# Gated MLP of an encoder layer: the down projection by Strassen's scheme, seven products for eight, with block sums on GpSimd

## The chip, the cores and the metric

The kernel runs on one core of a Trainium2 chip. The metric is the device time of one execution in microseconds (us). The core has a matrix engine (TensorE; PE in the profile, and PEld for its weight loads), VectorE (DVE), ScalarE (ACT), GpSimd (POOL), SyncE (SP), which issues the loads, and sixteen DMA engines. Every engine takes its own instructions in their order and waits for the others by semaphores.

## The reference

Two layers (`DEPTH = 2`) over 512 positions of width 1024; each has attention beside a gated convolution, a gated MLP, and an embedding gate. The change touches the last line of the MLP:

```python
h = rmsnorm(x, g_ffn[i])
u = dwconv(h @ w_up[i], w_ffn_conv[i])        # width 2 * D_FF, D_FF = 2816
a, val = u[..., :D_FF], u[..., D_FF:]
x = x + (jax.nn.silu(a) * val) @ w_down[i]    # (512, 2816) @ (2816, 1024)

h = rmsnorm(x, g_ple[i])
pg = jax.nn.sigmoid((h @ w_ple_gate[i]).astype(jnp.float32)).astype(x.dtype)
x = x + pg * (p[i] @ w_ple[i])
```

All is float32. The kernel gets near that precision by splitting each operand into a rounded high part and the rest (`split`, `weight`) and taking three products for one (`mm3`: high by high, high by low, low by high).

## The kernel before

**Tiles.** The residual stream `xs` stays in SBUF as 4 tiles of 128 tokens. The normed stream is transposed into `hh` and `hl` (high and low), hidden rows on the partitions. Every weight is loaded as 128x1024 numbers (512 KB) into `raw` (3 buffers); ScalarE casts it to `wh` and VectorE writes the rest into `wl` (5 buffers each, used in turn). So a weight's split has to wait until the tile that used the buffer five weights earlier is multiplied.

**Up projection.** The 22 blocks of 128 hidden columns are taken in order `j`. Each needs two weight tiles (`i = 2j` for the gate, `2j + 1` for the value) and for each 8 x 3 matmuls of 128x512 into a PSUM tile, `ps_mm` and `ps_sc` in turn (two buffers each): I call these 24 matmuls an up tile. `taps` makes the width 3 convolution of it (one ScalarE and two VectorE instructions, into `fa`), ScalarE applies Silu to the gate, VectorE multiplies both and the result is split into `gth` and `gtl`.

**Down projection.** `CHUNKS` cuts the 22 blocks into 8, 8 and 6. After the up tiles of a chunk `proj` runs over the two halves of 512 output columns and the four token tiles; for each it adds up `len(ks)` x 3 matmuls in one PSUM tile (`ps_tp`, three buffers, in the last chunk `ps_mm` and `ps_sc`), and `residual` adds the tile to `xs` on VectorE. In the last chunk `norm` follows for each token tile, whose square root is the only GpSimd work of this part.

**Order.** The program is written as loops, and a scheduler with a model of the engines' times then sets each engine's order. TensorE therefore runs parts of a later up tile or token tile ahead of a wait where the scheduler saw one. PSUM tiles and SBUF buffers of one tag are used in turn.

Of the kernel before, what the change touches and what calls it, by code (L numbers as in the profile page):

```python
# [11 lines left out]
F32 = mybir.dt.float32  # L12
F32R = mybir.dt.float32r
BF16 = mybir.dt.bfloat16
I32 = mybir.dt.int32
AF = mybir.ActivationFunctionType
ALU = mybir.AluOpType
AX = mybir.AxisListType

P = 128  # L20
L = 2
S = 512
NT = S // P
D = 1024
KD = D // P
# [10 lines left out]
FF = 2816  # L36
NJ = FF // P
EPS = 1e-6
CHUNKS = ((0, 8), (8, 16), (16, 22))
MAGIC = 12582912.0  # L40
LAG1 = 2
LAG2 = 3
# [16 lines left out]
def encoder_kernel(ctx, tc, x_in, pT, pos, inv, w_a1, w_z, w_g, w_uq, w_ukv, w_au, w_cu, w_o,  # L59
# [15 lines left out]
    def psum(tag="mm"):  # L75
        return ps.tile([P, S], F32, tag=tag, name="ps_" + tag, bufs={"mm": 2, "av": 1, "sc": 2, "tp": 3}[tag])

    def weight(src, n=1024):
        raw = wp.tile([P, n], F32, tag="raw", name="raw", bufs=3)
        nc.sync.dma_start(raw, src)  # L80
        h = wp.tile([P, n], F32R, tag="wh", name="wh")
        lo = wp.tile([P, n], F32R, tag="wl", name="wl")
        nc.scalar.copy(h, raw)  # L83
        nc.vector.tensor_sub(lo, raw, h.bitcast(F32))  # L84
        return h, lo

    def mm3(o, st, mv, start, stop):
        nc.tensor.matmul(o, st[0], mv[0], start=start, stop=False)  # L88
        nc.tensor.matmul(o, st[0], mv[1], start=False, stop=False)  # L89
        nc.tensor.matmul(o, st[1], mv[0], start=False, stop=stop)  # L90

    def split(hi, lo, src):
        nc.scalar.copy(hi, src)  # L93
        nc.vector.tensor_sub(lo, src, hi.bitcast(F32))  # L94
# [19 lines left out]
    def norm(t, g, pool):  # L114
        junk = pool.tile([P, D], BF16, tag="junk", name="junk", bufs=1)
        ms = sm.tile([P, 1], F32, tag="ms", name="ms")
        nc.scalar.activation(junk, xs[:, t, :], AF.Square, scale=1.0 / 32.0, accum_out=ms)  # L117
        r = rsqrt_eps(ms, 1)
        for half in range(2):
            c = slice(half * 512, half * 512 + 512)  # L120
            ht = pool.tile([P, 512], F32, tag="ht", name="ht", bufs=3)
            nc.vector.scalar_tensor_tensor(ht, xs[:, t, c], r, g[:, c], ALU.mult, ALU.mult)
            tp = psum("tp")
            for j in range(4):
                nc.tensor.transpose(tp[:, j * P:(j + 1) * P], ht[:, j * P:(j + 1) * P], ident)  # L125
            dst = (slice(None), t, slice(half * 4, half * 4 + 4), slice(None))
            split(hh[dst], hl[dst], tp.rearrange("p (j q) -> p j q", j=4))
# [60 lines left out]
    def layer(l, first):  # L188
# [69 lines left out]
        def ws(o, w, rhs, nk, width, off, cols=slice(0, S), ks=None):  # L258
            for k in range(nk) if ks is None else ks:
                c = slice(k * width + off, k * width + off + P)  # L260
                mm3(o, (w[0][:, c], w[1][:, c]), (rhs[0](k, cols), rhs[1](k, cols)), k == 0, k == nk - 1)
# [249 lines left out]
        def proj(lhs, ks, ws_, after, tags):  # L511
            for n in range(2):
                wt = [weight(ws_[n * (KTOT // 2) + k // 2]) for k in ks if k % 2 == 0]
                for t in range(NT):
# [5 lines left out]
                        mm3(o, (lhs[0](k, tk), lhs[1](k, tk)), (wh[:, c], wl[:, c]), i == 0, i == len(ks) - 1)  # L520
                    after(t, n, o)

        def residual(t, n, o):
            c = slice(n * 512, n * 512 + 512)
            nc.vector.tensor_tensor(xs[:, t, c], xs[:, t, c], o, ALU.add)  # L525
# [17 lines left out]
        def taps(i, o):  # L543
            a = t2("fa")
            nc.scalar.activation(a, o, AF.Copy, scale=wfc[:, i, 1:2])
            nc.vector.scalar_tensor_tensor(a[:, 1:], o[:, :-1], wfc[:, i, 0:1], a[:, 1:], ALU.mult, ALU.add)
            nc.vector.scalar_tensor_tensor(a[:, :-1], o[:, 1:], wfc[:, i, 2:3], a[:, :-1], ALU.mult, ALU.add)  # L547
            return a

        KTOT = NJ  # L550
        NE = 3
        ew = [weight(w_up[l, i]) for i in range(NE)]
        eo = [psum("sc" if i % 2 else "mm") for i in range(NE)]
# [2 lines left out]
            for i in range(NE):  # L556
                ws(eo[i][:, c], ew[i], hT, KD, P, 0, c)
        g3 = load_gain(l, 2, ff)
        for j0, j1 in CHUNKS:
            gt = {}  # L560
            for j in range(j0, j1):
                av = []
                for i in (2 * j, 2 * j + 1):
                    if i < NE:
                        o = eo[i]
                    else:
                        w = weight(w_up[l, i])
                        o = psum("sc" if i % 2 else "mm")
                        ws(o, w, hT, KD, P, 0)
                    a = taps(i, o)  # L570
                    if i % 2 == 0:
                        nc.scalar.activation(a, a, AF.Silu)  # L572
                    av.append(a)
                nc.vector.tensor_tensor(av[1], av[0], av[1], ALU.mult)  # L574
                if j % 2 == 0:
                    gt[j // 2] = (ff.tile([P, 2, S], F32R, tag="gt", name="gth", bufs=16),
                                  ff.tile([P, 2, S], F32R, tag="gt", name="gtl", bufs=16))
                split(gt[j // 2][0][:, j % 2, :], gt[j // 2][1][:, j % 2, :], av[1])

            def after_d(t, n, o, last=(j1 == NJ)):  # L580
                residual(t, n, o)
                if last and n == 1:
                    norm(t, g3, ff)

            proj((lambda k, c: gt[k // 2][0][:, k % 2, c], lambda k, c: gt[k // 2][1][:, k % 2, c]),
                 range(j0, j1), w_down[l], after_d, ("mm", "sc") if j1 == NJ else ("tp",))

        ph = ff.tile([P, 2, S], F32R, tag="gt", name="ph", bufs=16)
        pl = ff.tile([P, 2, S], F32R, tag="gt", name="pl", bufs=16)
        raw = wp.tile([P, 1024], F32, tag="raw", name="raw", bufs=3)  # L590
        nc.sync.dma_start(raw, pT[l])
        split(ph, pl, raw.rearrange("p (k s) -> p k s", k=2))
        pw = [ff.tile([P, D], F32, tag="gt", name="pw", bufs=16) for t in range(NT)]

        KTOT = 2

# [32 lines left out]
def _layout(i):  # L629
    f = {n: np.asarray(a) for n, a in i.items()}  # L630
    w_in = f["w_in"]
    o_cb, o_cc, o_cx, o_g = A1, A1 + CW, A1 + 2 * CW, A1 + 3 * CW

    def mtiles(w):
        l, k, n = w.shape
        return w.reshape(l, k // P, P, n // P, P).transpose(0, 3, 2, 1, 4)

    def interleave(*ws):
        return np.stack([mtiles(w) for w in ws], 2)

    def halves(w):
        l, k, n = w.shape
        return w.reshape(l, k // 256, 2, P, 2, 512).transpose(0, 4, 1, 3, 2, 5).reshape(l, k // 128, P, 1024)

    z = interleave(w_in[:, :, o_cc:o_cx], w_in[:, :, o_cx:o_g], w_in[:, :, o_cb:o_cc])
    g = interleave(w_in[:, :, o_g:o_g + D], w_in[:, :, o_g + D:])
    uq = f["w_uq"].reshape(L, QL, H, DQK)
    uq = np.concatenate([uq[..., :DN].reshape(L, QL, H * DN), uq[..., DN:].reshape(L, QL, H * DR)], -1)
    ukv = f["w_ukv"].reshape(L, KVL, H, 2, 64).transpose(0, 1, 3, 2, 4).reshape(L, KVL, 1024)

    def up2(w):
        l, k, n = w.shape
        return w.reshape(l, k // P, P, n // 256, 256).transpose(0, 3, 2, 1, 4).reshape(l, n // 256, P, 1024)

    up = interleave(f["w_up"][:, :, :FF], f["w_up"][:, :, FF:])
    fc = f["w_ffn_conv"].reshape(L, 3, 2, NJ, P).transpose(0, 4, 3, 2, 1).reshape(L, P, 2 * NJ, 3)
    res = {
        "x": f["x"][0],
        "pT": f["p"][:, 0].transpose(0, 2, 1).reshape(L, 2, P, S).transpose(0, 2, 1, 3).reshape(L, P, 1024),
        "pos": f["positions"].reshape(NT, P).T.astype(np.int32),  # L660
        "inv": (np.float32(10000.0) ** (-np.arange(0, DR, 2, dtype=np.float32) / np.float32(DR)))[None],
        "w_a1": _ktile(w_in[:, :, :A1], 2).reshape(L, 4, P, 2 * A1),
        "w_z": z.reshape(L, 12, P, 1024),
        "w_g": g.reshape(L, 16, P, 1024),
        "w_uq": uq.reshape(L, 2, P, H * DQK),
        "w_ukv": ukv,
        "w_au": up2(f["w_attn_up"]),
        "w_cu": up2(f["w_conv_up"]),
        "w_o": halves(f["w_o"]),
        "w_up": up.reshape(L, 2 * NJ, P, 1024),  # L670
        "w_down": halves(f["w_down"]),
        "w_pg": halves(f["w_ple_gate"]),
        "w_ple": halves(f["w_ple"]),
        "b_gate": f["b_gate"].reshape(L, 16, P).transpose(0, 2, 1),
        "g_norm": np.stack([f["g_mix"], f["g_ffn"], f["g_ple"]], 1),
        "g_lat": np.concatenate([f["g_q_lat"], f["g_kv_lat"]], 1),
        "g_nope": np.stack([f["g_q_head"][:, :DN], f["g_k_head"][:, :DN]], 2),
        "g_rope": np.stack([f["g_q_head"][:, DN:], f["g_k_head"][:, DN:]], 1),
        "w_conv": f["w_conv"].reshape(L, 3, NC, P).transpose(0, 3, 2, 1),
        "w_fconv": fc,  # L680
    }
    return {n: np.ascontiguousarray(a) for n, a in res.items()}
# [18 lines left out]
```

## Time and profile before

| | us |
|---|---|
| median of 3 timed runs | 1575.96 (1575.94 to 1576.26) |
| span of the profiled execution, first to last instruction | 1574.1 |
| PE busy / PEld busy | 1557.1 / 1280.1 |
| DVE busy / ACT busy / POOL busy | 870.4 / 684.4 / 103.0 |
| share of PE in the chain that ended last | 94% |
| MLP of the first layer in the span | about 375 to 740 |

The page gives the profiled execution's span and not the little that lies around it; I take the 1.9 us between the span and the median for that. A busy time counts a stretch in which an engine had any instruction running; matmuls follow each other before the one ahead has ended. In rows in order of time, the first number is the start in us from the span's start, the second the duration; brackets hold the idle time of that engine ahead and what ended it. In rows of one line's instructions, the three numbers after the count are shortest, median and longest duration in ns.

### The profile page before, as it was taken

How to read it: one execution, taken by the hardware profiler on the slowest of the kernel's cores; microseconds unless marked ns; L12 is line 12 of the kernel's file. 1: busy time of each engine (PE TensorE's matmuls, PEld its weight loads, DVE VectorE, ACT ScalarE, POOL GpSimd, SP SyncE). 2: the span in 40 equal slices, each digit the busy share in tenths (PEclk: the TensorE clock that was granted, in tenths of full speed). 3: DMA queues.
4: the chain of work that ended last, by engine and by line, in shares of the span. 5: the costliest groups of instructions: out<-in, count | busy, mean ns of one | idle time of the engine just before them, and what ended most of it. 6: DMA issues, size and time to landing. Idle time of an engine off the chain costs nothing.

```text
span 1574.1 us, 18521 instructions
## 1 busy us (share of the span) xinstructions
PE 1557.1 (99%) x7288; PEld 1280.1 (81%) x7288; DVE 870.4 (55%) x1228; ACT 684.4 (43%) x1088; POOL 103.0 (7%) x153
## 2 busy tenths in 40 slices
PE   7999999999999999999999999999999999999998
PEld 6888888888888888888888888888888888888886
DVE  7787553436544553555477775443565446535543
ACT  5678732325322431334464886222344234324342
POOL 2800000000000000001055000000000000000010
PEclk9999999999999999999999999999999999999999
DMA  6211122323213221323242102232232222232222
GB/s 205 93 55 41 54 94 94 106 69 129 95 61 130 93 95 58 132 96 94 71 133 81 41 28 92 81 107 81 85 118 94 94 94 94 80 107 94 94 68 79
DMA packets 41430, 142.06 MB, mean 90 GB/s; under 512 B 5761, under 2 KB 6273, under 8 KB 41345
## 3 DMA queue, kind: packets, MB, share of 16 engines
q1 hardware_dynamic: 41344, 140.90, 27.2%
q8 instruction: 57, 0.93, 0.2%
q14 instruction: 29, 0.23, 0.0%
HBM read 138.78 MB, written 2.10 MB: 90 GB/s over the span
## 4 chain that ended last, share of the span: by engine, by line
PE 94%; POOL 2%; DVE 2%; ACT 1%; DMA 1%; issue 1%; SPq 0%; DVEq 0%; POOLq 0%; ACTq 0%
PE ps_mm L89 14%; PE ps_mm L88 14%; PE ps_mm L90 14%; PE ps_sc L89 11%; PE ps_sc L88 11%; PE ps_sc L90 11%; PE ps_tp L89 4%; PE ps_tp L88 4%; PE ps_tp L90 4%; PE ps_tp L428 2%; PE ps_tp L125 1%; POOL rs L99 1%; PE ps_av L440 1%; PE ps_av L439 1%; PE ps_tp L394 1%; PE ps_av L88 1%
## 5 line engine op out<-in xcount | busy, mean ns | idle before, releaser
L84 DVE TENSOR_TENSOR wl<-raw,wh 128x1024 fp32r<-128x1024 f32 (+1 forms) x250 | 304.0, 1217 | 325.1 <-ACT wh L83 322.7
L83 ACT CAST wh<-raw 128x1024 fp32r<-128x1024 f32 (+1 forms) x250 | 260.8, 1046 | 425.6 <-PE ps_tp L90 120.3
L88 PE MATMUL ps_mm<-hh,wh 128*128 128x512 f32 (+1 forms) x832 | 326.4, 392 | 0.5 <-DVE ycv L355 0.5
L89 PE MATMUL ps_mm<-hl,wh 128*128 128x512 f32 (+1 forms) x832 | 322.9, 388 | 0.0
L90 PE MATMUL ps_mm<-hh,wl 128*128 128x512 f32 (+1 forms) x832 | 322.5, 388 | 0.0
L90 PEld LDWEIGHTS ps_mm<-hh,wl 128*128 128x128 f32 x832 | 156.6, 188 | 34.7
L88 PEld LDWEIGHTS ps_mm<-hh,wh 128*128 128x128 f32 x832 | 156.7, 188 | 33.2 <-DVE ycv L355 1.0
L89 PEld LDWEIGHTS ps_mm<-hl,wh 128*128 128x128 f32 x832 | 156.9, 189 | 32.5 <-DVE hl L94 0.4
L89 PE MATMUL ps_sc<-hl,wh 128*128 128x512 f32 (+1 forms) x368 | 142.2, 386 | 0.0
L90 PE MATMUL ps_sc<-hh,wl 128*128 128x512 f32 (+1 forms) x368 | 142.2, 386 | 0.0
L88 PE MATMUL ps_sc<-hh,wh 128*128 128x512 f32 (+1 forms) x368 | 142.1, 386 | 0.0
L98 POOL TENSOR_SCALAR ms<-ms 128x1 f32<-128x1 f32 (+2 forms) x40 | 15.8, 394 | 1389.0 <-ACT junk L117 1360.0
L89 PE MATMUL ps_tp<-wl,gth 128*128 128x512 f32 x256 | 100.6, 396 | 0.0
L90 PE MATMUL ps_tp<-wh,gtl 128*128 128x512 f32 x256 | 100.6, 395 | 0.0
L88 PE MATMUL ps_tp<-wh,gth 128*128 128x512 f32 x256 | 99.9, 395 | 0.0
L88 PEld LDWEIGHTS ps_sc<-hh,wh 128*128 128x128 f32 x368 | 69.3, 188 | 15.3
L90 PEld LDWEIGHTS ps_sc<-hh,wl 128*128 128x128 f32 x368 | 69.3, 188 | 15.3
L89 PEld LDWEIGHTS ps_sc<-hl,wh 128*128 128x128 f32 x368 | 69.3, 188 | 15.3
L93 ACT CAST gth<-fa 128x512 fp32r<-128x512 f32 x44 | 27.3, 620 | 120.1 <-DVE fa L574 120.1
L525 DVE TENSOR_TENSOR xs<-xs,ps_tp 128x512 f32<-128x512 f32 x32 | 21.6, 685 | 85.0 <-PE ps_tp L90 85.0
L572 ACT ACTIVATE fa<-fa 128x512 f32<-128x512 f32 x44 | 27.8, 632 | 88.5 <-DVE fa L547 88.5
L88 PEld LDWEIGHTS ps_tp<-wh,gth 128*128 128x128 f32 x256 | 48.1, 188 | 11.6
(242 smaller groups left out, 2671.2 us busy)
## 6 DMA issues: line engine op xcount, KB each, us to landing
raw<-in_w_up_dram SPq DMA_DIRECT2D x88, 512.0 KB, 3.5
raw<-in_w_down_dram SPq DMA_DIRECT2D x44, 512.0 KB, 3.4
raw<-in_w_g_dram SPq DMA_DIRECT2D x32, 512.0 KB, 3.5
raw<-in_w_z_dram SPq DMA_DIRECT2D x24, 512.0 KB, 3.5
raw<-in_w_o_dram SPq DMA_DIRECT2D x16, 512.0 KB, 3.5
raw<-in_w_pg_dram SPq DMA_DIRECT2D x16, 512.0 KB, 4.2
raw<-in_w_au_dram SPq DMA_DIRECT2D x8, 512.0 KB, 3.5
raw<-in_w_cu_dram SPq DMA_DIRECT2D x8, 512.0 KB, 3.5
```

What stands on the lines that cost most here:

```text
L83: nc.scalar.copy(h, raw)
L84: nc.vector.tensor_sub(lo, raw, h.bitcast(F32))
L88: nc.tensor.matmul(o, st[0], mv[0], start=start, stop=False)
L89: nc.tensor.matmul(o, st[0], mv[1], start=False, stop=False)
L90: nc.tensor.matmul(o, st[1], mv[0], start=False, stop=stop)
L93: nc.scalar.copy(hi, src)
L98: nc.gpsimd.tensor_scalar_add(ms, ms, EPS)
L99: nc.gpsimd.tensor_tensor(r, ms, negh[:, :n], ALU.pow)
L125: nc.tensor.transpose(tp[:, j * P:(j + 1) * P], ht[:, j * P:(j + 1) * P], ident)
L428: nc.tensor.transpose(tp[:, k * P:(k + 1) * P], pe[:, k * P:(k + 1) * P], ident)
L525: nc.vector.tensor_tensor(xs[:, t, c], xs[:, t, c], o, ALU.add)
L572: nc.scalar.activation(a, a, AF.Silu)
```

## The change

The first two blocks of a layer are projected as before. The other 20 form five chunks of four. In a chunk the left matrix is cut into token halves (256 tokens) and row halves (blocks 0 and 2, blocks 1 and 3: `v[:, 0]`, `v[:, 1]` of each pair), the weights into row and column halves (`b11` to `b22`). Seven products of 256 tokens, two row blocks and 512 columns replace eight. Their operands are:

- `combos`: per pair of blocks four sums of 128x256 on GpSimd (`ss`), two of which need the one before them, and the splits of three plain and four summed operands into `ah` and `al`;
- `seven`: four sums of 128x1024 on GpSimd over the weight tiles (`t3` and in place in `b12`, `b11`, `b21`), seven weight splits, then the products in the order `r2`, `r1`, `r3`, and accumulated further `r1`, `r3`, `r1`, `r1`. The state after a product is added to `xs` each time it is an output's share, so `residual` runs 14 times a chunk.

`r2` and `r3` lie in one `ps_tp` and the one `ps_av` tile, `r1` in two `ps_tp` tiles (in the last chunk `ps_sc` and `ps_mm`). The host stores `w_down` in the blocks that `seven` loads; the bytes loaded are the same.

```diff
-CHUNKS = ((0, 8), (8, 16), (16, 22))
+CHUNKS = ((0, 2), (2, 6), (6, 10), (10, 14), (14, 18), (18, 22))
+HS = S // 2
...
+        def combos(pool, v):
+            a11, a12, a21, a22 = v[:, 0, :HS], v[:, 1, :HS], v[:, 0, HS:], v[:, 1, HS:]
+            s = pool.tile([P, 4, HS], F32, tag="ss", name="ss", bufs=2)
+            g = nc.gpsimd
+            g.tensor_tensor(s[:, 0], a21, a22, ALU.add)
+            g.tensor_tensor(s[:, 2], a11, a21, ALU.subtract)
+            g.tensor_tensor(s[:, 1], s[:, 0], a11, ALU.subtract)
+            g.tensor_tensor(s[:, 3], a12, s[:, 1], ALU.subtract)
+            h, lo = (pool.tile([P, 7, HS], F32R, tag="gt", name=n, bufs=8) for n in ("ah", "al"))
+            split(h[:, 0:2], lo[:, 0:2], v[:, :, :HS])
+            split(h[:, 2], lo[:, 2], a22)
+            split(h[:, 3:], lo[:, 3:], s)
+            return h, lo
...
+        def seven(pool, ops, blocks, add, done, tags):
+            b11, b12, b21, b22 = (pool.tile([P, 1024], F32, tag="rawd", name=n, bufs=5)
+                                  for n in ("b11", "b12", "b21", "b22"))
+            for i, b in ((2, b21), (0, b11), (1, b12), (3, b22)):
+                nc.sync.dma_start(b, blocks[i])
+            t3 = pool.tile([P, 1024], F32, tag="rawd", name="t3", bufs=5)
+            g = nc.gpsimd
+            w21 = wsplit(b21)
+            w11 = wsplit(b11)
+            g.tensor_tensor(t3, b22, b12, ALU.subtract)
+            g.tensor_tensor(b12, b12, b11, ALU.subtract)
+            wt1 = wsplit(b12)
+            g.tensor_tensor(b11, b11, t3, ALU.add)
+            wt2 = wsplit(b11)
+            g.tensor_tensor(b21, b21, b11, ALU.subtract)
+
+            def product(o, a, w, first):
+                for tt in range(2):
+                    tk = slice(tt * P, (tt + 1) * P)
+                    for i, (h, lo) in enumerate(ops):
+                        c = slice(i * 512, i * 512 + 512)
+                        mm3(o[tt], (h[:, a, tk], lo[:, a, tk]), (w[0][:, c], w[1][:, c]),
+                            first and i == 0, i == len(ops) - 1, not first)
...
+            r2 = [psum(tags[2]), psum(tags[3])]
+            product(r2, 1, w21, True)
+            out(r2, 0, 0)
+            r1 = [psum(tags[0]), psum(tags[1])]
+            product(r1, 0, w11, True)
+            out(r1, 0, 0)
+            r3 = [psum(tags[2]), psum(tags[3])]
+            product(r3, 3, wt1, True)
+            out(r3, 1, 1)
+            product(r1, 4, wt2, False)
+            out(r1, 0, 1)
+            w22 = wsplit(b22)
+            product(r3, 6, w22, False)
...
+            if c:
+                seven(ff, ops, w_down[l, 4 * c - 2:4 * c + 2], residual,
+                      (lambda t: norm(t, g3, ff)) if last else (lambda t: None),
+                      ("mm", "mm", "sc", "sc") if last else ("tp", "tp", "tp", "av"))
```

What this makes of the engines' orders is shown for the end of a chunk's up tiles, the place on which the prediction rests. First TensorE before, in the down projection of the first chunk: `gth_3894` and `gtl_3895` are the last pair of blocks. The rows are numbers 42 to 49 of its matmuls.

```order
L90 MATMUL ps_tp_4022<-wh_3992,gtl_3895 128x512
L88 MATMUL ps_tp_4048<-wh_3974,gth_3475 128x512
L88 MATMUL ps_tp_3996<-wh_3992,gth_3894 128x512 [waits Activation_49]
L89 MATMUL ps_tp_3996<-wl_3993,gth_3894 128x512
L88 MATMUL ps_tp_4022<-wh_3992,gth_3894 128x512
L90 MATMUL ps_tp_3996<-wh_3992,gtl_3895 128x512 [waits DVE_49]
L89 MATMUL ps_tp_4022<-wl_3993,gth_3894 128x512
L90 MATMUL ps_tp_4022<-wh_3992,gtl_3895 128x512
```

TensorE now, in the second chunk of four (the others of a layer but the last have the same order): `ps_tp_4403` and `ps_av_4404` are `r2`, `ps_tp_4419` and `ps_tp_4420` are `r1`, `ps_tp_4435` is the first tile of `r3`; `ah_4366` and `al_4367` belong to the last pair of blocks, `ah_4208` to the pair before it. The first two rows are matmuls 11 and 12 of the products.

```order
L90 MATMUL ps_tp_4420<-wl_4388,ah_4208 128x512
L91 MATMUL ps_tp_4420<-wh_4387,al_4209 128x512
L89 MATMUL ps_tp_4403<-wh_4383,ah_4366 128x512 [waits Activation_49]
L90 MATMUL ps_tp_4403<-wl_4384,ah_4366 128x512
L89 MATMUL ps_av_4404<-wh_4383,ah_4366 128x512
L90 MATMUL ps_av_4404<-wl_4384,ah_4366 128x512
L89 MATMUL ps_tp_4419<-wh_4387,ah_4366 128x512
```

Eight rows on, the low part of the pair is read, and then the third product begins:

```order
L91 MATMUL ps_tp_4403<-wh_4383,al_4367 128x512 [waits DVE_49]
L91 MATMUL ps_av_4404<-wh_4383,al_4367 128x512
L91 MATMUL ps_tp_4419<-wh_4387,al_4367 128x512
L91 MATMUL ps_tp_4420<-wh_4387,al_4367 128x512
L89 MATMUL ps_tp_4435<-wh_4393,ah_4208 128x512 [waits DVE_49]
L90 MATMUL ps_tp_4435<-wl_4394,ah_4208 128x512
```

The last pair is wanted after 12 matmuls instead of after 43, and the 25th opens `r3` with a wait for VectorE. VectorE at the same two places, before and now; `fa_3965` and `fa_4356` are the taps of the last up tile, `wl_4103` and `wl_4466` weights for later:

```order
L84 TENSOR_TENSOR wl_4103<-raw_4100,wh_4102 128x1024 [waits DMAHW6_49,PE_49,Activation_49]
L546 SCALAR_TENSOR_TENSOR fa_3965<-ps_sc_3940,wfc_3296,fa_3965 128x511 [waits Activation_49]
L547 SCALAR_TENSOR_TENSOR fa_3965<-ps_sc_3940,wfc_3296,fa_3965 128x511 [waits DVE_49]
L574 TENSOR_TENSOR fa_3965<-fa_3929,fa_3965 128x512 [waits DVE_49]
L94 TENSOR_TENSOR gtl_3895<-fa_3965,gth_3894 128x512 [waits Activation_49]
L525 TENSOR_TENSOR xs_70<-xs_70,ps_tp_3996 128x512 [waits PE_49]
```

```order
L95 TENSOR_TENSOR wl_4466<-b22_4377,wh_4465 128x1024 [waits DMAHW2_49,PE_49,Activation_49]
L620 SCALAR_TENSOR_TENSOR fa_4356<-ps_sc_4331,wfc_3296,fa_4356 128x511 [waits Activation_49]
L621 SCALAR_TENSOR_TENSOR fa_4356<-ps_sc_4331,wfc_3296,fa_4356 128x511 [waits DVE_49]
L645 TENSOR_TENSOR gv_4216<-fa_4320,fa_4356 128x512 [waits DVE_49]
L95 TENSOR_TENSOR al_4367<-gv_4216,ah_4366 128x512 [waits Activation_49]
L95 TENSOR_TENSOR al_4367<-gv_4216,ah_4366 128x256 [waits Activation_49]
L95 TENSOR_TENSOR al_4367<-ss_4361,ah_4366 128x1024 [waits Activation_49]
L599 TENSOR_TENSOR xs_70<-xs_70,ps_tp_4403 128x512 [waits PE_49]
```

Up to the product of both taps the order is the same; then three splits stand in place of one ahead of the first residual add, and the third reads the GpSimd sums `ss_4361`. ScalarE has, in this order, the cast of `b22`, the taps of the last up tile, and the three casts into `ah_4366`.

More of the change, by code (lines that the diff above doesn't have):

```diff
@@ L85, in weight, with mm3 @@
         return h, lo
[L87 to L90, printed above, removed]
+    def mm3(o, st, mv, start, stop, more=False):
+        nc.tensor.matmul(o, st[0], mv[0], start=start, stop=False, skip_group_check=more)
+        nc.tensor.matmul(o, st[0], mv[1], start=False, stop=False, skip_group_check=more)
+        nc.tensor.matmul(o, st[1], mv[0], start=False, stop=stop, skip_group_check=more)
     def split(hi, lo, src):
@@ new lines, in wsplit, with out @@
+        def wsplit(raw):
+            h = wp.tile([P, 1024], F32R, tag="wh", name="wh")
+            lo = wp.tile([P, 1024], F32R, tag="wl", name="wl")
+            split(h, lo, raw)
+            return h, lo
+        def seven(pool, ops, blocks, add, done, tags):
[20 more added lines that the diff above has]
+                            first and i == 0, i == len(ops) - 1, not first)
+            def out(o, rows, n):
+                for tt in range(2):
+                    add(2 * rows + tt, n, o[tt])
+            r2 = [psum(tags[2]), psum(tags[3])]
[11 more added lines that the diff above has]
+            product(r3, 6, w22, False)
+            out(r3, 0, 1)
+            done(0)
+            done(1)
+            wt3 = wsplit(t3)
+            product(r1, 5, wt3, False)
+            out(r1, 1, 1)
+            wt4 = wsplit(b21)
+            product(r1, 2, wt4, False)
+            out(r1, 1, 0)
+            done(2)
+            done(3)
@@ L548, in taps @@
             return a
-        KTOT = NJ
         NE = 3
@@ L558, in layer @@
         g3 = load_gain(l, 2, ff)
[L559 to L586, printed above, removed]
@@ L588, in layer, with gated @@
-        ph = ff.tile([P, 2, S], F32R, tag="gt", name="ph", bufs=16)
-        pl = ff.tile([P, 2, S], F32R, tag="gt", name="pl", bufs=16)
+        def gated(j, v):
+            av = []
+            for i in (2 * j, 2 * j + 1):
+                if i < NE:
+                    o = eo[i]
+                else:
+                    w = weight(w_up[l, i])
+                    o = psum("sc" if i % 2 else "mm")
+                    ws(o, w, hT, KD, P, 0)
+                a = taps(i, o)
+                if i % 2 == 0:
+                    nc.scalar.activation(a, a, AF.Silu)
+                av.append(a)
+            nc.vector.tensor_tensor(v[:, j % 2, :], av[0], av[1], ALU.mult)
@@ new lines, in layer @@
+        for c, (j0, j1) in enumerate(CHUNKS):
+            ops = []
+            for j in range(j0, j1, 2):
+                v = ff.tile([P, 2, S], F32, tag="gv", name="gv", bufs=2)
+                gated(j, v)
+                gated(j + 1, v)
+                if c:
+                    ops.append(combos(ff, v))
+                else:
+                    gh, gl = (ff.tile([P, 2, S], F32R, tag="gt", name=n, bufs=8) for n in ("gh", "gl"))
+                    split(gh, gl, v)
+            last = j1 == NJ
+            if c:
+                seven(ff, ops, w_down[l, 4 * c - 2:4 * c + 2], residual,
+                      (lambda t: norm(t, g3, ff)) if last else (lambda t: None),
+                      ("mm", "mm", "sc", "sc") if last else ("tp", "tp", "tp", "av"))
+            else:
+                KTOT = 2
+                proj((lambda k, q: gh[:, k, q], lambda k, q: gl[:, k, q]), range(2), w_down[l], residual, ("tp",))
@@ L590, in layer @@
+        ph = ff.tile([P, 2, S], F32R, tag="gt", name="ph", bufs=8)
+        pl = ff.tile([P, 2, S], F32R, tag="gt", name="pl", bufs=8)
         raw = wp.tile([P, 1024], F32, tag="raw", name="raw", bufs=3)
@@ L592, in layer @@
         split(ph, pl, raw.rearrange("p (k s) -> p k s", k=2))
-        pw = [ff.tile([P, D], F32, tag="gt", name="pw", bufs=16) for t in range(NT)]
+        pw = [ff.tile([P, D], F32, tag="gt", name="pw", bufs=8) for t in range(NT)]
         KTOT = 2
@@ L653, in up2, with quads @@
         return w.reshape(l, k // P, P, n // 256, 256).transpose(0, 3, 2, 1, 4).reshape(l, n // 256, P, 1024)
+    def quads(w):
+        l, k, n = w.shape
+        w = w.reshape(l, k // 512, 2, 2, P, 2, 512)
+        return w.transpose(0, 1, 3, 5, 4, 2, 6).reshape(l, k // 128, P, 1024)
+    down = f["w_down"]
     up = interleave(f["w_up"][:, :, :FF], f["w_up"][:, :, FF:])
@@ L670, in _layout @@
         "w_up": up.reshape(L, 2 * NJ, P, 1024),
-        "w_down": halves(f["w_down"]),
+        "w_down": np.concatenate([halves(down[:, :256]), quads(down[:, 256:])], 1),
         "w_pg": halves(f["w_ple_gate"]),
```

## The prediction

> **What bounds the kernel now.** I read the page's engine table first, then the list of waits of TensorE, then the instructions in order of time at the end of one up projection tile.
>
> ```profile
> span 1574.1 us, 18521 instructions
> PE 1557.1 (99%) x7288; PEld 1280.1 (81%) x7288; DVE 870.4 (55%) x1228; ACT 684.4 (43%) x1088; POOL 103.0 (7%) x153
> ...
> PE ps_tp L125 <- DVE ht L122: 8.5, 2, 7.6
> PE ps_mm L89 <- DVE wl L84: 1.3, 3, 0.9
> ...
> 505.00:640.00 135.00, 135.00 (x579) 108.60 (x578) 68.45 (x81) 44.66 (x57) 0.00 (x0) 1.00 0.29 94
> ```
>
> TensorE is busy 99% of the span and hardly waits: 8.5 us for the first normed tile and 1.3 us for weights are its largest waits. In the second chunk of the MLP (505 to 640 us; PE, PEld, DVE, ACT, POOL busy, then clock, DMA share and GB/s) it has no gap, VectorE is half free, ScalarE two thirds free and GpSimd idle. So a matmul taken out is worth its time, and any wait put in front of TensorE is paid in full. The busy time of one matmul (0.39 to 0.40 us) is not its price, since matmuls overlap; the price is the step from start to start:
>
> ```profile
> 445.39 0.39 PE L88 MATMUL ps_sc<-hh,wh 128*128 128x512 f32 x1
> ...
> 451.01 0.40 PE L88 MATMUL ps_tp<-wh,gth 128*128 128x512 f32 x1
> ...
> 460.81 0.63 PE L88 MATMUL ps_tp<-wh,gth 128*128 128x512 f32 x2
> ```
>
> The first row opens the last up tile of the first chunk, the second opens its down projection: 24 matmuls in 5.62 us, 0.234 us each. The 42 after it take 9.80 us, the same 0.233.
>
> **What is removed.** Per layer the down projection had 22 row blocks x 4 token blocks x 2 halves x 3 = 528 matmuls. Now it has 48 for the plain first chunk and 5 x 7 products x 12 = 420: 468. Over two layers 120 are gone: 120 x 0.234 = 28.1 us. Nothing on TensorE is added, and the products are of the same 128x512 shape.
>
> **What is added beside the path.** Residual adds rise from 24 to 78 a layer, weight splits from 22 to 37, and the splits of the activations grow.
>
> ```profile
> L84 DVE TENSOR_TENSOR wl<-raw,wh 128x1024 fp32r<-128x1024 f32 (+1 forms) x250 | 304.0, 1217 | 325.1 <-ACT wh L83 322.7
> L83 ACT CAST wh<-raw 128x1024 fp32r<-128x1024 f32 (+1 forms) x250 | 260.8, 1046 | 425.6 <-PE ps_tp L90 120.3
> ...
> L525 DVE TENSOR_TENSOR xs<-xs,ps_tp 128x512 f32<-128x512 f32 x32 | 21.6, 685 | 85.0 <-PE ps_tp L90 85.0
> ```
>
> VectorE gets 54 x 0.685 + 15 x 1.217 = 55 us a layer and about 9 us for the larger activation splits; ScalarE 15 x 1.046 = 16 us and about 8. The MLP has some 350 us a layer, where VectorE now has half its time free, so as throughput this costs nothing. The w_down loads stay 22 a layer but go to `b11` to `b22`, whose next load waits on the sync queue until VectorE and GpSimd are done with the old tiles, with later w_up loads queued behind. That wait ends when `b21` has been split for the last product, by the timeline below about 15 us after a chunk's products begin; the first load behind it is used by the fourth up tile of the next chunk, 156 matmuls and the new waits later, at about 42 us.
>
> ```profile
> raw<-in_w_up_dram SPq DMA_DIRECT2D x88, 512.0 KB, 3.5
> ```
>
> Five loads of 3.5 us take 17.5 us of these 27: nothing.
>
> **What is added on the path.** Set zero at TensorE's first product matmul of a chunk (451.01 above). The last gated block is finished only after that, by a chain whose order on ScalarE and VectorE is the same before and after:
>
> ```profile
> 450.98 1.05 ACT L83 CAST wh<-raw 128x1024 fp32r<-128x1024 f32 x1 [1.14 <-PE ps_sc L89]
> 451.94 0.68 ACT L545 ACTIVATE fa<-ps_sc,wfc 128x512 f32<-128x512 f32 x1
> 452.06 1.23 DVE L84 TENSOR_TENSOR wl<-raw,wh 128x1024 fp32r<-128x1024 f32 x1 [2.95 <-ACT wh L83]
> 453.21 0.74 DVE L546 SCALAR_TENSOR_TENSOR fa<-ps_sc,wfc,fa 128x511 f32<-128x511 f32 x1
> 453.99 0.75 DVE L547 SCALAR_TENSOR_TENSOR fa<-ps_sc,wfc,fa 128x511 f32<-128x511 f32 x1
> 454.77 0.69 DVE L574 TENSOR_TENSOR fa<-fa 128x512 f32<-128x512 f32 x1
> 455.50 0.62 ACT L93 CAST gth<-fa 128x512 fp32r<-128x512 f32 x1 [2.88 <-DVE fa L574]
> 456.15 0.69 DVE L94 TENSOR_TENSOR gtl<-fa,gth 128x512 fp32r<-128x512 f32 x1 [0.69 <-ACT gth L93]
> ```
>
> A weight tile's cast and its subtraction stand ahead of the taps on both engines, because the buffer they fill is released by that same up tile. The cast of the block ends at 456.12, 5.1 us after zero, its low part at 5.8.
>
> Wait A. Before, 43 other product matmuls came first (10 us), so this was hidden. Now a chunk of four has one other pair of blocks, and TensorE's row shows 12 matmuls ahead of the first that reads `ah_4366`: due at 12 x 0.234 = 2.8 us, possible at 5.15. Cost 2.35 us per chunk.
>
> Wait B. The third product starts 24 matmuls in, due at 5.6 us, after wait A at 7.95. Its PSUM tile is the one of the first product (three `tp` tiles), so it waits for the residual add of `ps_tp_4403`. In VectorE's order that add stands behind the low part of the four sums (`al_4367<-ss_4361`), and that behind ScalarE's cast of them and the four GpSimd sums, which can start when the block is multiplied, at 455.46, 4.5 us after zero. So a sum that is not needed until later holds up an add whose input is ready.
>
> How long is a 128x256 sum on GpSimd? The trace has none so wide; it has narrower ones:
>
> ```profile
> L252 POOL TENSOR_TENSOR kr<-ra,rb x8: 215/223/1245, 59.8 to 821.2; 128x16 f32<-128x16 f32 x8
> L252 POOL TENSOR_TENSOR qc<-ra,rb x8: 456/465/1382, 60.6 to 856.7; 128x128 f32<-128x128 f32 x8
> L242 POOL TENSOR_TENSOR sg<-sinT,grope x8: 321/326/1122, 45.6 to 810.0; 128x64 f32<-128x64 f32 x8
> ...
> 70.90 0.26 POOL L250 TENSOR_TENSOR ra<-krope,cg 128x32 f32<-128x32 f32 x1
> 71.11 1.29 POOL L251 TENSOR_TENSOR rb<-krope,sg 128x32 f32<-128x32 f32 x1
> ...
> 71.08 1.21 DVE L84 TENSOR_TENSOR wl<-raw,wh 128x1024 fp32r<-128x1024 f32 x1
> ```
>
> The shortest ones (first number) give (456 - 215) / 112 = 2.15 ns a column and 0.18 us fixed: 0.73 us for 256 columns. From below I bound it by the 128 column sum itself (0.46), from above by twice that (0.92). The two 32 column rows show the other thing that counts: 0.26 us alone, 1.29 when a VectorE subtraction with both inputs in SBUF has just begun. In our chain VectorE runs two such subtractions (512 and 256 columns) from 5.1 to about 6.2 us, over the second sum. Four sums with two gaps of 0.08 us end at 7.5 us without a collision; if the second sum is held until 6.2, at 8.5. I take 8.0. Then ScalarE's cast starts at 8.05, VectorE's subtraction 1.08 later as above (452.06 - 450.98) and takes 1.23, to 10.35; the add ends 0.65 later, near 10.95; TensorE goes on at 11.0. Due 5.6, so A and B together cost 5.4 us, between 4.9 and 5.9.
>
> [...]
>
> After that TensorE runs through: the other adds of the first two products must be done by 12.4, 13.8 and 15.2 us (six matmuls, 1.4 us, apart), and VectorE, with one weight split between them, has done them by about 11.6, 12.2 and 13.9.
>
> The last chunk of a layer has another order: there the add of the first product stands ahead of the sums' low part, behind the subtraction for `pl`, so TensorE starts the third product at 8.35, then waits for the sums' cast (9.65 if the sums end at 8.5) and has done 34 matmuls at 11.3 instead of 7.95: 3.4 us, between 2.7 and 4.1.
>
> The 1024 column sums of weights (0.18 + 1024 x 2.15 ns = 2.4 us, four per chunk) run while up tiles are multiplied, one or more tiles before their casts; hidden. If VectorE were held by them for more than the one up tile (5.6 us) by which PSUM is doubled, TensorE would stop there too.
>
> **The sum.** Eight chunks of the middle kind and two last ones: 8 x 5.4 + 2 x 3.4 = 50.0 us of new waiting, less 28.1: 22 us slower. The span of 1574.1 becomes 1596; the median of the timed runs, 1575.96, is 1.9 above the span, so I say 1598. The bounds of the collisions give 8 x 4.9 + 2 x 2.7 = 44.6 and 8 x 5.9 + 2 x 4.1 = 55.4: 1592 to 1603. The bounds of one sum (0.46 and 0.92 us, four in each chain) move it by -1.1 and +0.8 us a chunk, so 1587 and 1606 about the middle, 1582 to 1611 if both ends meet.
>
> **Rivals.**
>
> The clock. TensorE stands still about 2.35 and 3.05 us in each chunk, and after a longer stop it was slow:
>
> ```profile
> 9.93 0.55 PE L89 MATMUL ps_mm<-wl,hh 128*128 128x416 f32 x1
> 10.28 0.58 PE L90 MATMUL ps_mm<-wh,hl 128*128 128x416 f32 x1
> ...
> 16.74 0.46 PE L89 MATMUL ps_mm<-wl,hh 128*128 128x416 f32 x1 [0.88 <-DVE wl L84]
> 17.03 0.35 PE L90 MATMUL ps_mm<-wh,hl 128*128 128x416 f32 x1
> 17.22 0.35 PE L88 MATMUL ps_mm<-wh,hh 128*128 128x416 f32 x1
> ```
>
> After the 7.6 us start the step was 0.35 us, after a stop of 0.88 us it was 0.19 at once. The spell at the start lasts from 9.4 to about 14 us; at half speed that is 2.1 us lost. If every chunk paid this, 10 x 2.1 = 21 us more: 1619. The two stops lie between the lengths shown, nearer to the harmless one, and 2.8 us of work parts them. [...] Chance 0.14.
>
> Another wait: the wide weight sums, or the sync queue behind `b21`, hold up a weight split that TensorE needs, 1 to 2 us a chunk: 1608 to 1618. For it speaks that GpSimd is given about 15 us of work a chunk (8 x 0.73 + 4 x 2.4), in a fixed order; against it that the up tiles have two PSUM tiles and five weight buffers. Chance 0.12.
>
> Faster: the sums come in time. TensorE would wait only for A if the add were done by 7.95, which needs the four sums to end 0.5 us after their start: 10 x 2.35 = 23.5 against 28.1, 1571. The change breaks even at 2.8 us a chunk, so at sums of 0.2 us each; the 16 column sum already takes 0.215. Chance 0.05, with it that a matmul is worth more than its step.
>
> No effect, the waits just eating the gain (1573 to 1579): 0.03. The forecast itself: 0.66.
>
> **Range and chances.** A measurement of this kernel can tell about 0.2%, 3 us. The range takes the bounds of the sums and of the collisions and reaches into the clock's case: 1584 to 1619. Faster 0.05, same 0.03, slower 0.92.
>
> **What would show it.** In the profile after: 7168 matmuls; in the list of waits, TensorE waiting for the cast `ah` about 2.3 us, ten times, and for the residual add (`xs`, or named by its PSUM tile) about 3 us, eight times; GpSimd sums of 256 columns near 0.73 us, the second of a chain longer; a clock of 1.00. It would be wrong if sums are not late, if VectorE's add is not behind them, or if the clock drops.

## The result and the profile after

| | us | ratio to the kernel before, 95% interval |
|---|---|---|
| before | 1575.95 | |
| changed kernel, median (4 runs) | 1599.45 (1597.0 to 1600.99) | 1.0148 [1.0133, 1.0162] |
| its profiled execution | 1597.0, span 1595.2, mean granted clock 0.991 | |

The kernel became 23.5 us slower; 1598 was forecast. Of the four executions of the first experiment's kernel below, one ran at under half the clock throughout (3340 us, mean granted clock 0.456) and is left out of that experiment's numbers. The page of the changed kernel, then its list of TensorE's waits (engine, tile and line that waited, what it waited for; us in total, times, longest):

```profile
span 1595.2 us, 18618 instructions
PE 1547.1 (97%) x7168; PEld 1263.9 (79%) x7168; DVE 1040.9 (65%) x1384; ACT 726.7 (46%) x1136; POOL 286.9 (18%) x273
```

```profile
PE ps_tp L89 <- ACT ah L94: 17.6, 8, 2.2
PE ps_tp L126 <- DVE ht L123: 8.9, 2, 8.0
PE ps_tp L89 <- DVE xs L599: 8.7, 7, 2.1
PE ps_sc L89 <- DVE fa L621: 3.2, 2, 1.6
PE ps_mm L90 <- DVE wl L85: 1.3, 3, 0.9
```

The 120 matmuls are gone. The second and fifth row stood in the kernel before too (8.5 and 1.3). The first is wait A, in eight chunks, the third wait B, in seven. But waits A and B and the fourth row sum to 29.5 us, and the loss is 21.1 us of span plus the 28.1 saved, 49.2. The rest doesn't show as waiting: matmuls were slower for a while. One chunk of the first layer in order of time, ScalarE, VectorE, GpSimd and TensorE:

```profile
439.90 0.39 PE L89 MATMUL ps_tp<-wh,ah 128*128 128x512 f32 x1
...
442.46 0.40 PE L91 MATMUL ps_tp<-wh,al 128*128 128x512 f32 x1
...
443.65 0.69 DVE L645 TENSOR_TENSOR gv<-fa 128x512 f32<-128x512 f32 x1
444.38 0.92 ACT L94 CAST ah<-gv 128x512 fp32r<-128x512 f32 x2 [2.88 <-DVE gv L645]
444.42 0.73 POOL L528 TENSOR_TENSOR ss<-gv 128x256 f32<-128x256 f32 x1 [8.49 <-DVE gv L645]
445.03 1.57 DVE L95 TENSOR_TENSOR al<-gv,ah 128x512 fp32r<-128x512 f32 x2 [0.68 <-ACT ah L94]
...
445.05 0.50 PE L89 MATMUL ps_tp<-wh,ah 128*128 128x512 f32 x1 [2.19 <-ACT ah L94]
...
445.23 1.09 POOL L530 TENSOR_TENSOR ss<-ss,gv 128x256 f32<-128x256 f32 x1
...
446.40 0.80 POOL L531 TENSOR_TENSOR ss<-gv,ss 128x256 f32<-128x256 f32 x1
...
447.23 1.04 ACT L94 CAST ah<-ss 128x1024 fp32r<-128x1024 f32 x1 [1.93 <-POOL ss L531]
...
448.31 1.23 DVE L95 TENSOR_TENSOR al<-ss,ah 128x1024 fp32r<-128x1024 f32 x1 [1.71 <-ACT ah L94]
...
449.45 0.68 DVE L599 TENSOR_TENSOR xs<-xs,ps_tp 128x512 f32<-128x512 f32 x1
...
450.19 0.50 PE L89 MATMUL ps_tp<-wh,ah 128*128 128x512 f32 x1 [0.93 <-DVE xs L599]
```

The first product starts at 439.90. TensorE stops after its twelfth matmul and goes on 5.15 us after zero, as forecast. The third product starts 10.29 us after zero instead of 5.6: 4.7 us, and the step that a stop is left by costs 0.1 more. Its wait is listed with 0.93 us only, because the matmuls ahead of it ran at half speed. Here is the granted clock by the microsecond (third column from the end), and then wait B in a later chunk (the third of the layer), with a matmul from the spell at half clock that follows it there:

```profile
446.00:447.00 1.00, 1.00 (x6) 0.80 0.00 0
447.00:448.00 1.00, 1.00 (x4) 0.50 0.00 0
...
449.00:450.00 1.00, 0.26 (x1) 0.50 0.00 0
```

```profile
588.08 0.68 DVE L599 TENSOR_TENSOR xs<-xs,ps_tp 128x512 f32<-128x512 f32 x1
...
588.81 0.50 PE L89 MATMUL ps_tp<-wh,ah 128*128 128x512 f32 x1 [2.08 <-DVE xs L599]
...
590.58 0.63 PE L89 MATMUL ps_av<-wh,ah 128*128 128x512 f32 x1
```

At half clock the step from start to start is 0.427 us instead of 0.234. In the first chunk that lies inside wait B, whose end VectorE sets, and costs nothing. In the later chunk the spell (590.0 to 593.4) comes after wait B, and costs 1.6 us on top.

To add this up I took all steps of TensorE's rows in order of time that are longer than 0.234 us, by chunk, in us lost:

| chunk (time of its first stop) | 442 | 512 | 581 | 652 | 721 last | 1231 | 1298 | 1369 | 1438 | 1508 last |
|---|---|---|---|---|---|---|---|---|---|---|
| lost | 4.8 | 4.8 | 6.4 | 4.8 | 3.6 | 2.8 | 6.4 | 4.8 | 6.3 | 4.4 |

That is 48.9 us before rounding; less 28.1 it gives 20.8, against 21.1 measured between the spans. The chunk at 1231 has no wait B. There the scheduler placed the adds ahead of the sums' subtraction on VectorE:

```profile
1235.39 1.05 ACT L94 CAST ah<-ss 128x1024 fp32r<-128x1024 f32 x1 [1.93 <-POOL ss L531]
...
1235.61 0.69 DVE L599 TENSOR_TENSOR xs<-xs,ps_tp 128x512 f32<-128x512 f32 x1 [0.86 <-PE ps_tp L91]
1236.21 0.68 DVE L599 TENSOR_TENSOR xs<-xs,ps_av 128x512 f32<-128x512 f32 x1
1236.35 0.51 PE L89 MATMUL ps_tp<-wh,ah 128*128 128x512 f32 x1
...
1236.81 1.22 DVE L95 TENSOR_TENSOR al<-ss,ah 128x1024 fp32r<-128x1024 f32 x1
```

The add runs as soon as its PSUM tile is done, and the third product follows 0.7 us later with no wait listed.

### The profile page after: what moved, and what is told of

Same layout as the page of the kernel before. It is cut to its first block, busy times and chain, and to the rows that moved or that the text cites. A ratio compares the mean times of both kernels' runs of the same rounds, so it can differ in the third digit from the quotient of the medians.

```text
span 1595.2 us, 18618 instructions
## 1 busy us (share of the span) xinstructions
PE 1547.1 (97%) x7168; PEld 1263.9 (79%) x7168; DVE 1040.9 (65%) x1384; ACT 726.7 (46%) x1136; POOL 286.9 (18%) x273
## 4 chain that ended last, share of the span: by engine, by line
PE 88%; DVE 5%; POOL 3%; ACT 2%; issue 1%; DMA 0%; DVEq 0%; POOLq 0%; ACTq 0%
PE ps_mm L90 14%; PE ps_mm L89 14%; PE ps_mm L91 14%; PE ps_sc L89 10%; PE ps_sc L90 10%; PE ps_sc L91 10%; PE ps_tp L89 3%; PE ps_tp L90 2%; PE ps_tp L91 2%; PE ps_tp L429 2%; PE ps_av L89 1%; PE ps_av L90 1%; PE ps_av L91 1%; PE ps_tp L126 1%; POOL rs L100 1%; PE ps_av L441 1%
## 5 line engine op out<-in xcount | busy, mean ns | idle before, releaser
L84 ACT CAST wh<-raw 128x1024 fp32r<-128x1024 f32 (+1 forms) x210 | 219.1, 1046 | 415.8 <-PE ps_mm L90 125.0
L85 DVE TENSOR_TENSOR wl<-raw,wh 128x1024 fp32r<-128x1024 f32 (+1 forms) x210 | 273.6, 1304 | 198.0 <-ACT wh L84 191.5
L95 DVE TENSOR_TENSOR wl<-b,wh 128x1024 fp32r<-128x1024 f32 x60 | 82.5, 1375 | 74.9 <-ACT wh L94 74.9
L89 PE MATMUL ps_tp<-wh,ah 128*128 128x512 f32 x176 | 73.4, 417 | 26.3 <-ACT ah L94 17.6
L599 DVE TENSOR_TENSOR xs<-xs,ps_tp 128x512 f32<-128x512 f32 x104 | 69.9, 681 | 21.3 <-PE ps_tp L91 20.9
L94 ACT CAST wh<-b 128x1024 fp32r<-128x1024 f32 x60 | 62.8, 1047 | 44.1 <-PE ps_sc L90 22.1
L90 PE MATMUL ps_tp<-wl,ah 128*128 128x512 f32 x176 | 72.3, 411 | 0.0
L91 PE MATMUL ps_tp<-wh,al 128*128 128x512 f32 x176 | 70.1, 406 | 0.0
```

The lines of the kernel that those rows point to most:

```text
L89: nc.tensor.matmul(o, st[0], mv[0], start=start, stop=False, skip_group_check=more)
L90: nc.tensor.matmul(o, st[0], mv[1], start=False, stop=False, skip_group_check=more)
L91: nc.tensor.matmul(o, st[1], mv[0], start=False, stop=stop, skip_group_check=more)
```

## Experiments

**The adds first.** The one chunk is an accident of the scheduler; the first run makes that order in all chunks.

```diff
-            split(h[:, 3:], lo[:, 3:], s)
...
+            if not defer:
+                split(h[:, 3:], lo[:, 3:], s)
...
+            r2done = out(r2, 0, 0)
...
+            h, lo, s = ops[-1]
+            with tc.issue_after(r2done[1].ins):
+                split(h[:, 3:], lo[:, 3:], s)
...
```

`defer` is true for the last pair of a chunk, and `r2done[1]` is the second of the first product's two adds.

> The subtraction of the sums of a chunk's last pair is queued on VectorE behind both residual adds of the first product; no instruction is added or taken away. Theory (the add sits behind that subtraction): seven chunks lose wait B, 2.3 us each with what stands around it, and keep wait A of 2.5; a chunk then costs about 2.8 us of waiting like the one of the second layer that has this order already. The 49 us of the changed kernel shrink by 7 x 1.9 to about 35, less where half clock was hidden by wait B: the half clock spells (1.6 us each) are no longer covered, so 8 to 16 us are gained: 1583 to 1592 us. Rival 1 (the sums themselves, not the order, hold TensorE: the third product's operands come from them): nothing gained, 1599. Rival 2 (the clock is the cost and the wait only its cover): 7 spells x 1.6 come out into the open and the gain is under 3 us, 1596 to 1600.

Measured: 1583.32 us (median of 1582.85, 1583.32 and 1586.07), 1.0054 [1.0034, 1.0075] of before and 16.1 us faster than the changed kernel; span 1581.5. No wait for `xs` with `ps_tp` is left:

```profile
PE ps_tp L89 <- ACT ah L94: 17.6, 8, 2.2
...
PE ps_sc L89 <- DVE fa L624: 3.2, 2, 1.6
```

Four middle chunks lose 2.8 us, and four 4.2 to 4.4, where a spell at half clock now stands uncovered. The sums and their cast on ScalarE keep their place: in the first chunk the cast starts 2.19 us after the end of wait A, against 2.18 in the changed kernel. So wait B is a matter of the order on VectorE; both rivals are out.

**The adds first, and wait A filled.** The same with 90 matmuls more.

```diff
-                        mm3(o[tt], (h[:, a, tk], lo[:, a, tk]), (w[0][:, c], w[1][:, c]),
-                            first and i == 0, i == len(ops) - 1, not first)
+                        for m in range(3 if a == 0 and tt and i == 0 else 0, -1, -1):
+                            mm3(o[tt], (h[:, a, tk], lo[:, a, tk]), (w[0][:, c], w[1][:, c]),
+                                first and i == 0, m > 0 or i == len(ops) - 1, not first)
```

> As the run with the adds first, and 9 matmuls a chunk more: the first six-operand part of the second tile of the second product is computed four times, each time from new, so that TensorE has 21 instead of 12 matmuls (4.9 us) ahead of the last pair; 90 matmuls, 21 us of TensorE work, that only fill wait A. Theory with the clock (a stop of 2.2 us inside a stretch of 3.4 us halves the clock for the next 3.4 us): the stops shrink to 0.3 to 0.4 us, the mean clock returns to 0.999, and the kernel is as fast as without the extra matmuls or faster by up to the spells, 1575 to 1588, lower than the run with the adds first by 0 to 12 us. Rival (the clock does not follow the stops): the spells stay, same time as the run with the adds first. Rival (the wait is not of fixed end but moves with TensorE's work): 21 us slower than it.

Measured: 1577.04 us, 1.0007 [0.9998, 1.0016]; span 1575.1. With 21 us more work for TensorE it is 6.3 us faster than the run before. The same three stretches of 10 us (PE busy, matmuls, clock), first with the adds first, then with the fill:

```profile
440.00:450.00 10.00, 7.73 (x33) 1.00 0.16 52
576.00:586.00 10.00, 7.80 (x26) 0.83 0.16 53
645.00:655.00 10.00, 7.71 (x26) 0.83 0.16 52
```

```profile
440.00:450.00 10.00, 9.83 (x42) 1.00 0.17 52
576.00:586.00 10.00, 9.82 (x41) 1.00 0.16 53
645.00:655.00 10.00, 9.82 (x42) 1.00 0.14 54
```

No spell at half clock is left (mean granted clock 1.0, against 0.995 in the run before): the clock followed the stops. And the wait has a fixed end, the cast of the last pair, so that work put into it is free: a middle chunk now loses 0.7 us.

**The sums on VectorE.** Do slow GpSimd sums make wait B?

```diff
-            g = nc.gpsimd
+            g = nc.vector
             g.tensor_tensor(s[:, 0], a21, a22, ALU.add)
...
-            out(r2, 0, 0)
+            if tags[0] == "mm" or (l, c) == (1, 1):
+                out(r2, 0, 0)
+            else:
+                with tc.issue_after(ops[-1][2]):
+                    out(r2, 0, 0)
```

The second cut puts the adds behind the sums' subtraction (`ops[-1][2]`), as in the changed kernel. It leaves out the last chunks and the second layer's first one (the chunk at 1231 above), where the order is the scheduler's.

> The four 128x256 sums of a pair of blocks on VectorE instead of GpSimd (the 128x1024 weight sums stay on GpSimd); the order of the residual adds behind the sums' subtraction is kept in all eight middle chunks. Theory (order): after the gated product VectorE needs two sums of about 0.42 us (half of 0.69 and a fixed part), the two subtractions 1.2, one sum 0.42, ScalarE's cast 1.05, the subtraction 1.2, the add 0.65: the third product starts 9.5 us after the first instead of 10.3. Seven chunks gain 0.7 us, the eighth, which had the other order, loses 1.1: 4 us gained, 1595 (1591 to 1598). Rival (slow GpSimd sums are the whole of wait B): 2.3 us a chunk gained, 1583. Rival (VectorE gets too full): over 1600.

Measured: 1590.27 us, 1.0091 [1.0076, 1.0106]. In order of time, with the first product at 439.81:

```profile
444.30 0.42 DVE L528 TENSOR_TENSOR ss<-gv 128x256 f32<-128x256 f32 x1
444.75 0.42 DVE L530 TENSOR_TENSOR ss<-ss,gv 128x256 f32<-128x256 f32 x1
...
446.49 1.05 ACT L94 CAST ah<-ss 128x1024 fp32r<-128x1024 f32 x1 [1.27 <-DVE ss L531]
...
449.44 0.50 PE L89 MATMUL ps_tp<-wh,ah 128*128 128x512 f32 x1 [1.41 <-DVE xs L602]
```

The third product starts 9.63 us after the first, not 10.29: 0.66 us, forecast 0.7. That is what quicker sums bring while cast and subtraction still stand ahead of the add. The gain, 9 us, is larger than the 4 forecast: the spells of half clock fell into other places (a chunk that had lost 6.4 now loses at most 5.1), and the two last chunks lose 2.9 each. The forecast left both out. In the chunk whose order was left open the scheduler put the adds behind the subtraction this time: it loses 4.1 us, as the expectation had assumed for it, instead of 2.8.

**The last sum three times.**

```diff
             g.tensor_tensor(s[:, 3], a12, s[:, 1], ALU.subtract)
+            g.tensor_tensor(s[:, 3], a12, s[:, 1], ALU.subtract)
+            g.tensor_tensor(s[:, 3], a12, s[:, 1], ALU.subtract)
...
```

The rest of the edit sets the order of the adds as in the run before.

> The last of the four GpSimd sums of a pair is computed three times (same result); the order on VectorE is kept as in the changed kernel for the middle chunks. Theory (sums, cast, subtraction and add in a row set when the third product starts): two sums of 0.80 us and two gaps of 0.08 put 1.75 us on wait B in each of the seven chunks that have it, and 0.7 to 1.75 in the other three: 12 to 18 us slower, 1612 to 1617. Rival (the sums are hidden, the wait has another cause, the clock or the weight splits): 1599 as before.

Measured: 1625.58 us, 1.0313 [1.0298, 1.0329]: 26 us slower than the changed kernel, more than forecast. In four of the seven chunks with wait B the orders are as before; there the third product starts 11.9 us after the first (588.88 to 600.79 in the third chunk of four), 1.6 later than without the added sums, as forecast. In the three others, and in the chunk without wait B, the scheduler also put two weight casts ahead of the cast of the sums on ScalarE, which the run was not meant to change:

```profile
521.27 0.73 POOL L533 TENSOR_TENSOR ss<-gv,ss 128x256 f32<-128x256 f32 x1
...
522.43 1.05 ACT L94 CAST wh<-t 128x1024 fp32r<-128x1024 f32 x1 [3.92 <-PE ps_av L91]
523.38 1.04 ACT L94 CAST wh<-b 128x1024 fp32r<-128x1024 f32 x1
524.33 1.04 ACT L94 CAST ah<-ss 128x1024 fp32r<-128x1024 f32 x1
...
526.92 0.68 DVE L604 TENSOR_TENSOR xs<-xs,ps_tp 128x512 f32<-128x512 f32 x1
```

The sums end at 522.00 and could have been cast then; their cast starts at 524.33. The longer stops also bring more half clock (mean 0.981). So only the start times in the four chunks answer the question: what is put into the chain ahead of the add arrives at TensorE in full.

**The products later.** If both waits are chains that need 5 to 10 us, 48 matmuls of the next chunk put ahead of them cover both.

```diff
                 gated(j, v)
+                if later:
+                    later.pop()()
                 gated(j + 1, v)
...
```

`later` holds the call of `seven` for the chunk before.

> The seven products of a chunk are issued behind the first two up tiles (48 matmuls, 11.2 us) of the next chunk, so that taps, sums, casts and subtractions of the last pair are done when TensorE comes to them; only the last chunk of a layer stays where it is. Nothing else is changed. Theory (waits A and B and the half clock they bring are chains that only need 5 to 10.3 us of cover): the eight middle chunks lose all their waiting, 41 of the 49 us; the two last chunks keep 8: 1558 us (1554 to 1563), faster than the kernel before by about 1.1%, clock 0.997 or more. Rival (the operations added on VectorE, ScalarE and GpSimd or the 37 weight splits through five buffers hold TensorE anyway): 1575 to 1595.

Measured: 1557.74 us, 0.9885 [0.9872, 0.9899]; span 1555.3. The eight middle chunks lose nothing, the last ones 4.8 us each. Sums, casts and subtractions take the same time as before (1.09 us for the second sum), but TensorE is elsewhere:

```profile
444.53 0.73 POOL L528 TENSOR_TENSOR ss<-gv 128x256 f32<-128x256 f32 x1 [3.33 <-DVE gv L645]
...
445.34 1.09 POOL L530 TENSOR_TENSOR ss<-ss,gv 128x256 f32<-128x256 f32 x1
446.51 0.80 POOL L531 TENSOR_TENSOR ss<-gv,ss 128x256 f32<-128x256 f32 x1
447.34 1.05 ACT L94 CAST ah<-ss 128x1024 fp32r<-128x1024 f32 x1 [0.39 <-POOL ss L531]
...
448.98 1.21 DVE L95 TENSOR_TENSOR al<-ss,ah 128x1024 fp32r<-128x1024 f32 x1
...
450.82 0.40 PE L89 MATMUL ps_tp<-wh,ah 128*128 128x512 f32 x1
```

**The plain blocks last.** Here the two blocks outside the scheme end the layer instead of opening it, and the last seven products stand between their up tiles and their plain projection.

```diff
-CHUNKS = ((0, 2), (2, 6), (6, 10), (10, 14), (14, 18), (18, 22))
+CHUNKS = ((0, 4), (4, 8), (8, 12), (12, 16), (16, 20), (20, 22))
...
+                later.pop()()
...
+                proj((lambda k, q: gh[:, k, q], lambda k, q: gl[:, k, q]), range(2), w_down[l, 20:], after_d, ("mm", "sc"))
...
```

> As the run with the products later, and the two blocks that are projected without the scheme are the last of a layer instead of the first: the last seven products stand between their up tiles and their plain projection, and cover that chain too. Theory: no wait of the scheme is left, 1599.4 - 49 = 1550 us (1547 to 1554), the 28 us of 120 matmuls fully gained against the kernel before. Rival (the end of the layer, where the norm waits for the last adds, costs what is gained): 1558 or more, no better than the run with the products later.

Measured: 1548.59 us, 0.9827 [0.9813, 0.984], the fastest of all. Its page and its longest waits:

```profile
span 1546.4 us, 18624 instructions
PE 1529.3 (99%) x7168; PEld 1257.0 (81%) x7168; DVE 1030.9 (67%) x1384; ACT 727.1 (47%) x1136; POOL 286.7 (19%) x273
```

```profile
PE ps_tp L126 <- DVE ht L123: 8.3, 2, 7.4
PE ps_mm L90 <- DVE wl L85: 1.3, 3, 0.9
```

No wait of the scheme is left, with the same matmuls and very nearly the same work on the other engines as in the changed kernel. Against the kernel before the span is 27.7 us shorter; 120 matmuls at 0.234 are 28.1.

**Small chunks, eight products.** The kernel before with only the new `CHUNKS`.

> The kernel before with chunks of 2, 4, 4, 4, 4 and 4 blocks in place of 8, 8 and 6; eight products, no sums. Residual adds rise from 24 to 48 a layer, matmuls stay 7288. Theory (wait A comes from the small chunk only together with the seven products' weight splits: here the order puts 27 product matmuls and 16 of the next up tile ahead of the last pair, 10 us): no new wait, 1576 us (1574 to 1580). Rival (a chunk of four alone brings wait A of 2.4 us, eight to ten times): 1595 to 1600.

Measured: 1578.1 us, 1.0014 [1.0005, 1.0023]. The smaller chunk by itself doesn't bring wait A: there the scheduler filled the wait with the next up tile's matmuls. In its first chunk of four, whose products begin at 439.71, 16 of them stand between the products of the other pair and the first one that reads the last pair, 10.0 us after zero:

```profile
446.01 0.40 PE L88 MATMUL ps_mm<-hh,wh 128*128 128x512 f32 x1
...
449.75 0.40 PE L88 MATMUL ps_tp<-wh,gth 128*128 128x512 f32 x1
```

In the changed kernel it did not. Seven weight splits through five pairs of buffers stand ahead of the next up tile's there, which may be why; a kernel with more such buffers, which could tell, was not run. Where the 2.1 us come from I have not traced.

## Why the prediction was right, point by point

- **The saving**, 28.1 us by the step of 0.234 us: 27.7 in the run with the plain blocks last.
- **Wait A**, 2.35 us: measured 2.36 and 0.1 for leaving it, in eight chunks. In the two last ones TensorE stops first, 1.6 us, for the taps of the last up tile (`fa`), since the products' `ps_sc` tile is the one that they read. The prediction had not seen that. It had 3.4 us for such a chunk, and they lost 3.6 and 4.4.
- **Wait B**, 3.05 us: mechanism right, size too large; at full clock it took 2.3 (2.24 and 0.1 for leaving it, in the third chunk). Of the four sums one needs only the first block of the pair and was done early (L529), so three stand in the chain, which ends at 7.3 us after zero, not 8.0; the third product started at 10.29, not 11.0. The plain sum took 0.73 us as worked out. The second took 1.09, starting 0.2 us after VectorE's subtraction with two SBUF inputs. The next subtraction, of 256 columns, started while that sum ran and took 0.96 us; in the run with the sums on VectorE it took 0.42. When the second sum began, some 0.49 of the first subtraction's 0.69 us were left, and the sum took 0.36 longer than the plain one. The rows show the overlaps and the longer times, not what ties them.
- **Eight chunks** with wait B: seven. The prediction took the order at one place for that of all.
- **The clock**, a rival at 0.14 with 21 us: it came, in eight chunks of ten, but cost some 5.5 us, in the three chunks at 6.3 to 6.4 and the last one at 4.4. Elsewhere it lay inside wait B. The price of a spell, 2.1 us, was too high: it is 1.6. "A clock of 1.00" was wrong: 0.991. The argument that the stops lie nearer to the harmless 0.88 us was a guess between far ends.
- **The sum**, 50.0 us of loss: 48.9. The middle chunks had 43.2 and took 41.0, the last ones 6.8 and took 7.9. Wait B smaller and once missing (about 8 us) and the clock's cost nearly cancel, so the total is closer than its terms, by luck.
- **Hidden work**: the weight sums (2.4 us forecast, 2.40 to 3.44 measured), loads and weight splits held TensorE nowhere, as the runs with the products later show.

## What to carry to other kernels

A step that saves work on the bounding engine pays only if what its operands pass through is covered (here 1599.45 us with the waits and 1548.59 without, against 1575.95 before): count the independent matmuls between the last producer and the first consumer, and put the consumer behind the next block of work if there are too few. Then ask, of the wait that is left, what stands ahead in the in-order queue of the engine that ends it; an add with its input ready waited here for a subtraction that nobody needed yet (in the third chunk of four its input was done at 586.03 and it began at 588.08, 2.05 us later). The list of waits understated such a wait where the clock dropped inside it (0.93 us listed of 2.2 in the first chunk of four), so compare start times, not waits.

## What the runs showed of the hardware

The clock halved without a long stop: in the chunks of the changed kernel none was over 2.2 us. I laid out the five profiles with such stops (the changed kernel, the adds first, the sums on VectorE, the last sum three times, the products later). In them half clock, between the kernel's start and its end, lasted 3.41 us or twice that, and its starts lay on a grid of 3.413 us within one execution (in the changed kernel 514.9, 590.0 and 1306.8 lie 20, 42 and 252 steps from the first, 446.6, to 0.1 us). I added up TensorE's stops over 0.3 us, from the end of one matmul to the start of the next, in each grid stretch. In all 31 stretches after which the clock dropped they came to at least 1.86 us; in the other stretches at full clock to at most 1.77. So in these runs the limit at full clock lay between 1.77 and 1.86 of 3.41 us, no sharper than the ends of matmuls, which the profile models. Two short stops in one stretch counted together: 1.61 and 0.35 us brought the changed kernel's drop at 1511.6, while a stop of 2.2 us in the run with the adds first, 1.77 of it in one stretch, brought none. By this it was phase that decided whether such a stop brought a spell, and up to 1.6 us more. The stops of the changed kernel's chunks never filled a stretch, 2.2 us of 3.41 at most, and the drop came.
